# Second mix: gate tiles interleaved with conv tiles; expert tables: one 512-column matmul for high and low x

## The chip, the cores and the metric

The kernel runs on one core of a Trainium2 chip. The metric is device time in microseconds of one execution, here the median of three. TensorE (PE) multiplies, with its weight loads shown apart (PEld); VectorE (DVE), ScalarE (ACT) and GpSimd (POOL) work on what it leaves; SyncE (SP) issues the weight transfers.

## What is computed

Two blocks on 256 tokens of 1024 features. Each has a mixer and then a product-key retrieval over 16384 single-neuron experts. The change touches the second mixer's input projection and the first expert table (`expert_u`) of both blocks:

```python
def second_block(x, ...):
    h = _rmsnorm(x, norm1)
    proj = h @ w_in
    a_q, a_k, a_v, a_beta, a_alpha, a_gate, b_f, b_i, b_q, b_gate, g_a, g_b = _split_cols(proj)
    qkv = _causal_conv_silu(concatenate([a_q, a_k, a_v]), conv_a)    # 4 taps
    o_a = _rmsnorm(_gated_delta_rule(qa, ka, va, beta, log_alpha), a_onorm) * silu(a_gate)
    f_gate = lb + (1.0 - lb) * sigmoid(b_f)
    o_b = _rmsnorm(_hgrn2_recurrence(silu(b_q), 1.0 - f_gate, b_i, log(f_gate)), b_onorm) * sigmoid(b_gate)
    mix = sigmoid(g_a) * (o_a @ w_branch_a) + sigmoid(g_b) * (o_b @ w_branch_b)
    x = x + mix @ w_out
    return x + _peer(_rmsnorm(x, norm2), ...)

def block(xt, it, gt):                       # _peer, for 128 tokens
    h = gelu(einsum('td,tkd->tk', xt, expert_u[it]))
    return einsum('tk,tkd->td', gt * h, expert_v[it])
```

## The kernel before

Both tables are computed densely: scores for all 128 x 128 experts, Gelu, and a gate that is zero where an expert was not chosen. All large products run in three parts, because operands are split into a high and a low piece: high x times high w, low x times high w, high x times low w. A weight tile is 128 x 1024 numbers. `_dma` (L141) fetches it on SP's queue into one of three buffers `raw`; `_conv` (L148) lets ScalarE make `hi` and VectorE or GpSimd make `lo`, cut at column `lo_cut`: VectorE has the columns below it, GpSimd the rest (`CUT` for the tables, `CUT2` for the second mix). `hi` and `lo` have three buffers each, so those of tile e+3 wait for the end of tile e.

`tile_ch` (L178) is one output tile of 128 channels by 256 tokens: for each of 8 chunks of 128 features three matmuls of 256 columns (L187), 24 in a row, into an accumulator `mm` of which there are two. Six more banks (y0 to y3, g0, g1, handed out by `bank`, L123) serve the work that runs beside the tiles.

In `Peer.run` (L552) the first table has 128 tiles, e = 0 to 127. After each, `gelu` (L540) applies the activation on ScalarE, and multiplies on VectorE where the gates are already there; `step` (L196) then lets the background advance by a budget of 1.6 us of estimated VectorE time: first the retrieval (`topk16`, L422, and one-hot rows), then `gates` (L504), which builds the gates by f16 matmuls (L527) of one-hot rows and writes or multiplies them into the scores (L533, L535).

`Mix2.run` (L1389) has 80 input tiles. Before: 24 conv tiles (for each of 8 heads q, k, v), then 8 tiles of the gate a, 8 of f, 8 of q of the second branch, 8 of its gate, 8 of its values, 16 of ga and gb. `conv` (L1006) empties the accumulator into `cvx` on ScalarE, then does three scalar-times-tensor-plus-tensor steps on VectorE (L1013), a sigmoid on ScalarE and a product on VectorE (L1017). `head` (L1019) transposes the result on TensorE (L1025) and takes norms. `both` (L1512) runs the delta rule for heads 0 to 3 and, when all conv tiles are out, for heads 4 to 7. Generators like these advance by a round per `pass_round`, two rounds after each tile.

The order on each engine is not the order of this code alone: a scheduler sets it from the program's dependences. The engines take their instructions strictly in that order.

Of the kernel before, what the change touches and what calls it, by code (L numbers as in the profile page):

```python
# [84 lines left out]
class K:  # L85
    def __init__(self, tc, ins, ctx, plan):
# [4 lines left out]
        self.xh = self.fix.tile([P, NC, T], FR, name="xh")  # L91
        self.xl = self.fix.tile([P, NC, T], FR, name="xl")
# [85 lines left out]
    def tile_ch(self, xh=None, xl=None):  # L178
# [4 lines left out]
        ps = self.ps.tile([P, T], F32, tag="mm", name="mm", bufs=2)  # L183
# [247 lines left out]
class Peer:  # L431
# [108 lines left out]
    def gelu(self, e, ps):  # L540

        nc, n = self.k.nc, self.gated
        a, s = (self.a0, e) if e < SPLIT else (self.a1, e - SPLIT)
        if n < T:
            nc.scalar.activation(out=a[:, s, n:T], in_=ps[:, n:T], func=ACTF.Gelu)  # L545
        if n:
            ge = self.oh.tile([P, T], F32, name="ge", tag="ah", bufs=AB)
            nc.scalar.activation(out=ge[:, 0:n], in_=ps[:, 0:n], func=ACTF.Gelu)
            nc.vector.tensor_tensor(out=a[:, s, 0:n], in0=a[:, s, 0:n], in1=ge[:, 0:n], op=ALU.mult)
        self.acted = e + 1  # L550

    def run(self, after):  # L552
# [3 lines left out]
        with ExitStack() as es:  # L556
# [66 lines left out]
            for e in range(P):  # L623
# [9 lines left out]
                self.gelu(e, k.tile_ch())  # L633
                k.step(BUD[0])
# [257 lines left out]
CUT2 = [384, 640]  # L892
# [9 lines left out]
class Mix2:  # L902
# [14 lines left out]
    def columns(self):  # L917
# [44 lines left out]
        yield  # L962
# [55 lines left out]

    def head(self, h, what, src):  # L1019

        k, nc = self.k, self.k.nc
# [12 lines left out]
        k.done(bt)  # L1034

    def delta(self, g4):
# [5 lines left out]
        ss = self.ssq[g4]  # L1042
        rr = self.t([P, 2, 2, 4], "rr", bufs=2)
# [37 lines left out]
        yield from self.blocks16(lt, X)  # L1081
        lv = self.lev_p.rearrange("p (l n) -> p l n", l=2)
# [306 lines left out]
    def run(self):  # L1389
# [34 lines left out]
        for h in range(H):  # L1424
            for what in range(3):
                ps = k.tile_ch()
                dst = self.t([P, T], "vc", tag="vc", bufs=2) if what == 2 else (self.qc, self.kc)[what][:, h, :]
                self.conv(ps, what * 8 + h, dst)
                k.spawn(self.head(h, what, dst))
                after(2)  # L1430
            if h == 3:
                k.spawn(self.both())
        self.ready.add("qkv")
        k.lo_cut = CUT2[1]
        for h in range(H):
            ps = k.tile_ch()
            silu(ps, self.sga[:, h, :], oa)
            after(2)
        self.ready.add("a_gate")
        for h in range(H):  # L1440
            ps = k.tile_ch()
            self.sigmoid(self.fs[:, h, :], ps)
            after(2)
        for h in range(H):
            ps = k.tile_ch()
            silu(ps, self.qb[:, h, :])
            after(2)
# [64 lines left out]
    def both(self):  # L1512
        yield from self.delta(0)
        while "qkv" not in self.ready:
            yield
# [25 lines left out]

def mix2_out_order():

    for j in range(10):
        if j < 8:
            yield "b", j
        if j > 1:
# [6 lines left out]
MIX2_COLS = ([w * 1024 + h * 128 for h in range(8) for w in range(3)]  # L1554
             + _PART(0) + _PART(1) + _PART(3) + _PART(4) + _PART(2) + _PART(5) + _PART(6))
# [80 lines left out]
```

## Time and profile before

| what | us |
|---|---|
| median of three executions (2248.23 to 2250.43) | 2250.25 |
| the profiled execution | 2248.88 |
| its span, first to last instruction | 2247.1 |
| TensorE busy | 2181.1 (97%) |
| VectorE busy | 1546.5 (69%) |
| ScalarE busy | 1166.4 (52%) |
| GpSimd busy | 829.3 (37%) |

A busy share is an average over stages with different limits. The first table of the first block runs from about 204 to 604 us of the span, that of the second from about 1491 to 1895; the second mix from 955 to 1430 us. Matmuls are pipelined: one has a duration of some 0.28 us, but the next may start 0.12 us later, so the rate is read from the starts, and a stretch that is busy all the time may still be stretched by a lower granted clock (PEclk).

### The profile page before, as it was taken

The page shows a single profiled execution, that of the slowest core. Times are in us where ns is not written, and L with a number is a line of the kernel's source. Part 1 is how long each engine was busy: PE and PEld are TensorE (multiplying, and loading weights), DVE is VectorE, ACT ScalarE, POOL GpSimd, SP SyncE. Part 2 cuts the span into 40 slices and gives each one's busy share as a digit, 9 for nine tenths or more (in the row PEclk, how much of TensorE's full clock was granted, in tenths as well). Part 3 has the DMA queues.
Part 4 walks back from the last instruction along what each step waited for, and adds up shares of the span by engine and source line. Part 5 has one row for each costly group of instructions (what it writes and reads, how often), then busy time and mean ns, then how long its engine had stood idle before and what let it go on. Part 6 is the DMA issues. An engine that isn't in the chain of part 4 may idle for free. (4 is left out here: it accounts for less than half of the span.)

```text
span 2247.1 us, 41435 instructions
## 1 busy us (share of the span) xinstructions
PE 2181.1 (97%) x15512; PEld 2025.8 (90%) x15512; DVE 1546.5 (69%) x3119; ACT 1166.4 (52%) x2210; POOL 829.3 (37%) x626
## 2 busy tenths in 40 slices
PE   8999999999999999988899999999999999999998
PEld 7989999999988888778899898899999999888887
DVE  5659986889544544579756787799778885454444
ACT  5645545444555555565444555455454445555554
POOL 3454000000166666645553675530000001656664
PEclk9999999999999999999999999999999999999999
DMA  5555655555556666633334244555555555666664
GB/s 187 158 172 167 183 174 162 159 160 160 178 191 202 205 191 196 187 101 119 123 104 136 64 132 140 178 165 185 171 168 154 157 160 180 195 204 191 195 195 153
DMA packets 103881, 370.90 MB, mean 165 GB/s; under 512 B 12928, under 2 KB 14080, under 8 KB 103424
## 3 DMA queue, kind: packets, MB, share of 16 engines
q1 hardware_dynamic: 101808, 365.21, 52.1%
q10 hardware_dynamic: 1872, 3.04, 0.4%
q8 instruction: 122, 2.00, 0.4%
q14 instruction: 79, 0.65, 0.1%
HBM read 367.16 MB, written 1.05 MB: 164 GB/s over the span
## 5 line engine op out<-in xcount | busy, mean ns | idle before, releaser
L157 POOL TENSOR_TENSOR lo<-raw,hi 128x384 fp32r<-128x384 f32 (+2 forms) x428 | 702.3, 1643 | 1337.3 <-ACT hi L152 1306.7
L152 ACT ACTIVATE hi<-raw 128x1024 fp32r<-128x1024 f32 x684 | 724.0, 1060 | 693.6 <-PE mm L187 405.9
L187 PE MATMUL mm<-xh,hi 128*128 128x256 f32 x3168 | 918.8, 290 | 15.5 <-ACT cvx L1009 5.7
L187 PE MATMUL mm<-xh,lo 128*128 128x256 f32 x3168 | 902.8, 285 | 0.4 <-DVE lo L157 0.4
L187 PE MATMUL mm<-xl,hi 128*128 128x256 f32 x3168 | 898.8, 284 | 1.3 <-DVE xl L309 1.0
L157 DVE TENSOR_TENSOR lo<-raw,hi 128x640 fp32r<-128x640 f32 (+2 forms) x654 | 665.9, 1019 | 336.1 <-ACT hi L152 331.8
L187 PEld LDWEIGHTS mm<-xh,hi 128*128 128x128 f32 x3168 | 603.4, 190 | 19.6 <-ACT cvx L1009 6.8
L187 PEld LDWEIGHTS mm<-xl,hi 128*128 128x128 f32 x3168 | 604.0, 191 | 2.7 <-DVE xl L309 1.6
L187 PEld LDWEIGHTS mm<-xh,lo 128*128 128x128 f32 x3168 | 599.8, 189 | 0.6 <-DVE lo L157 0.6
L261 PE MATMUL y<-lo,ah 128*128 128x512 f32 x1024 | 398.3, 389 | 0.0
L261 PE MATMUL y<-hi,ah 128*128 128x512 f32 x1024 | 397.4, 389 | 0.0
L261 PE MATMUL y<-hi,al 128*128 128x512 f32 x1024 | 276.0, 389 | 0.0
L617 DVE TENSOR_TENSOR al<-a,ah 128x256 fp32r<-128x256 f32 x256 | 118.7, 464 | 188.8 <-PE y L261 188.5
L261 PEld LDWEIGHTS y<-lo,ah 128*128 128x128 f32 x1024 | 192.2, 188 | 40.2 <-POOL lo L157 0.3
L261 PEld LDWEIGHTS y<-hi,al 128*128 128x128 f32 x1024 | 192.2, 188 | 39.8
L261 PEld LDWEIGHTS y<-hi,ah 128*128 128x128 f32 x1024 | 192.2, 188 | 39.8
L616 ACT ACTIVATE ah<-a 128x256 fp32r<-128x256 f32 x256 | 106.4, 416 | 167.2 <-PE y L261 165.7
L517 DVE TENSOR_TENSOR ow<-ow,w 128x1024 f16<-128x1024 f16 x128 | 87.3, 684 | 0.1
L545 ACT ACTIVATE a<-mm 128x256 f32<-128x256 f32 (+33 forms) x228 | 69.2, 303 | 0.0
L527 PEld LDWEIGHTS <-o 128*128 128x128 f16 x1024 | 59.6, 97 | 6.3
L514 DVE TENSOR_TENSOR ow<-iota,ij 128x1024 f16<-128x1024 f16 x64 | 44.3, 692 | 27.6 <-PE by L527 19.1
L533 DVE TENSOR_TENSOR a<-by,a 128x256 f32<-128x256 f32 (+15 forms) x144 | 47.8, 349 | 11.9 <-PE by L527 11.6
(500 smaller groups left out, 1972.1 us busy)
## 6 DMA issues: line engine op xcount, KB each, us to landing
raw<-in_u_dram SPq DMA_DIRECT2D x256, 512.0 KB, 3.6
raw<-in_v_dram SPq DMA_DIRECT2D x256, 512.0 KB, 4.2
raw<-in_w_in_dram SPq DMA_DIRECT2D x108, 512.0 KB, 3.6
raw<-in_wq_dram SPq DMA_DIRECT2D x32, 512.0 KB, 3.9
raw<-in_w_out_dram SPq DMA_DIRECT2D x16, 512.0 KB, 3.6
raw<-in_w_branch_a_dram SPq DMA_DIRECT2D x8, 512.0 KB, 3.5
raw<-in_w_branch_b_dram SPq DMA_DIRECT2D x8, 512.0 KB, 3.7
skT<-in_sk_dram ACTq DMA_DIRECT2D x2, 1024.0 KB, 5.2
```

Of the source, the lines that this page charges most:

```text
L152: self.nc.scalar.activation(out=h, in_=r, func=ACTF.Copy)
L157: eng.tensor_tensor(out=l[:, a:b], in0=r[:, a:b], in1=h[:, a:b].bitcast(F32), op=ALU.subtract)
L187: self.nc.tensor.matmul(out=ps, lhsT=a[:, c, :], rhs=b, start=(c == 0 and k == 0), stop=(c == NC - 1 and k == 2))
L261: i = self.nc.tensor.matmul(out=self.y[tt][dh], lhsT=p[:, ts], rhs=q[:, ds], start=(first and m == 0), stop=(last and m == 2))
L514: nc.vector.tensor_tensor(out=ow[0], in0=iota, in1=some(self.ij[:, 1]), op=ALU.is_equal)
L517: nc.vector.tensor_tensor(out=ow[q], in0=ow[0], in1=some(self.w[:, q]), op=ALU.mult)
L527: nc.tensor.matmul(out=g[:, n, :], lhsT=hot[n][0], rhs=hot[n][1 + q], start=(q == 0), stop=(q == 1))
L533: nc.vector.tensor_tensor(out=v, in0=gi[:, e:e + hi - lo], in1=v, op=ALU.mult)
L545: nc.scalar.activation(out=a[:, s, n:T], in_=ps[:, n:T], func=ACTF.Gelu)
L616: nc.scalar.activation(out=h, in_=a, func=ACTF.Copy)
L617: nc.vector.tensor_tensor(out=l, in0=a, in1=h.bitcast(F32), op=ALU.subtract)
```

## The change

*Expert tables.* `tile_pair` is a second form of a table tile. High and low x now stand side by side in one buffer `xx`, so one matmul of 512 columns multiplies a chunk of `hi` with both, into the two halves of a bank; one of 256 columns adds high x times `lo` to the first half. ScalarE copies the second half out, VectorE adds the first half to it, and Gelu reads the sum. It is used for every odd tile and for tiles after the background has run out; its step has 0.25 us less budget. The accumulator `mm` is now two whole banks.

*Second mix.* The 24 conv tiles and the 16 tiles of gate a and f come in one mixed order (`mix2_in_order`): a gate tile after every third conv tile for heads 0 to 3, then after every one. `tile_wide` takes one of the six banks as accumulator when at least four are free. `conv` no longer copies into `cvx`: ScalarE's scaled copy and VectorE's three steps read the accumulator itself. The sigmoid, the product and the transposes moved into `head`, behind two further rounds. The delta rule waits for its own heads, and blocks of four heads follow each other without the wait for all conv tiles. While these 40 tiles run, VectorE makes 640 columns of `lo` instead of 384 for the conv tiles. The columns of the weight in memory are permuted to the new order.

```diff
+        self.xx = self.fix.tile([P, NC, 2, T], FR, name="xx")
+        self.xh, self.xl = self.xx[:, :, 0, :], self.xx[:, :, 1, :]
...
+    def tile_pair(self):
+
+        h, l = (a.rearrange("p (c n) -> p c n", c=NC) for a in self.weights())
+        ps = self.ps.tile([P, 2, T], F32, tag="mm", name="mm", bufs=2)
+        for c in range(NC):
+            both = lambda: self.nc.tensor.matmul(out=ps.rearrange("p a t -> p (a t)"), lhsT=h[:, c, :], rhs=self.xx[:, c].rearrange("p a t -> p (a t)"),
+                                                 start=(c == 0), stop=(c == NC - 1))
+            if c < NC - 1:
+                both()
+            self.nc.tensor.matmul(out=ps[:, 0, :], lhsT=l[:, c, :], rhs=self.xh[:, c, :], start=False, stop=False)
+            if c == NC - 1:
+                both()
+        return ps
+
+    def tile_wide(self):
+
+        if len(self.free) < 4:
+            return self.tile_ch(), lambda: None
+        tag = self.free.popleft()
+        return self.tile_ch(tag=tag), lambda: self.done(tag)
...
+        if pair:
+            ps = self.k.tile_pair()
+            nc.scalar.activation(out=ge, in_=ps[:, 1], func=ACTF.Copy)
+            nc.vector.tensor_tensor(out=ge, in0=ps[:, 0], in1=ge, op=ALU.add)
+            ps = ge
+        else:
+            ps = self.k.tile_ch()
...
-                self.gelu(e, k.tile_ch())
-                k.step(BUD[0])
+                pair = e % 2 == 1 or not k.bg
+                self.gelu(e, pair)
+                k.step(BUD[0] - 0.25 * pair)
...
-CUT2 = [384, 640]
+CUT2 = [640, 640]
...
-    def conv(self, ps, n, out):
+    def conv(self, h, what):
+
         k, nc = self.k, self.k.nc
-        c = self.t([P, T], "cvx", tag="hon", bufs=2)
-        nc.scalar.activation(out=c, in_=ps, func=ACTF.Copy)
+        n = what * 8 + h
+        ps, done = k.tile_wide()
         a = self.t([P, T], "cva", tag="c0", bufs=3)
-        nc.scalar.activation(out=a, in_=c, func=ACTF.Copy, scale=self.cw[:, n, 3:4])
+        nc.scalar.activation(out=a, in_=ps, func=ACTF.Copy, scale=self.cw[:, n, 3:4])
         for s in (1, 2, 3):
-            nc.vector.scalar_tensor_tensor(out=a[:, s:T], in0=c[:, 0:T - s], scalar=self.cw[:, n, 3 - s:4 - s], in1=a[:, s:T],
+            nc.vector.scalar_tensor_tensor(out=a[:, s:T], in0=ps[:, 0:T - s], scalar=self.cw[:, n, 3 - s:4 - s], in1=a[:, s:T],
                                            op0=ALU.mult, op1=ALU.add)
+        done()
+        k.spawn(self.head(h, what, a))
+
+    def head(self, h, what, a):
+        k, nc = self.k, self.k.nc
+        yield
+        yield
         s = self.t([P, T], "cvs", tag="c1", bufs=2)
         self.sigmoid(s, a)
-        nc.vector.tensor_tensor(out=out, in0=a, in1=s, op=ALU.mult)
...
+        src = self.t([P, T], "vc", tag="vc", bufs=2) if what == 2 else (self.qc, self.kc)[what][:, h, :]
+        nc.vector.tensor_tensor(out=src, in0=a, in1=s, op=ALU.mult)
+        yield
...
+        while not all(("head", h, what) in self.ready for h in hs for what in range(3)):
+            yield
...
+    conv = [("c", h, what) for h in range(H) for what in range(3)]
+    rest = [("a", h, 0) for h in range(H)] + [("f", h, 0) for h in range(H)]
+    for n, c in enumerate(conv):
+        yield c
+        if n % 3 == 2 or n >= 12:
+            yield rest.pop(0)
```

The order, at three places. First VectorE in the first table, while the retrieval works on its candidates (`cand`, `ct`, `ci`); `lo` is the low piece of a weight tile. Before:

```order
L157 TENSOR_TENSOR lo_2798<-raw_2694,hi_2796 128x1024
L449 TENSOR_TENSOR cand_3013<-st_1728 128x1024 x2
L157 TENSOR_TENSOR lo_2835<-raw_2731,hi_2833 128x1024
L424 MAX ct_2648<-cand_3013 128x8 x8
L157 TENSOR_TENSOR lo_2872<-raw_2763,hi_2870 128x1024
L425 MAX_INDEX ci_2649<-ct_2648,cand_3013 128x8 x6
L157 TENSOR_TENSOR lo_2909<-raw_2800,hi_2907 128x1024
```

Now:

```order
L474 TENSOR_TENSOR cand_3036<-st_1727 128x1024 x2
L179 TENSOR_TENSOR lo_2809<-raw_2710,hi_2807 128x1024
L449 MAX ct_2637<-cand_3036 128x8 x4
L574 TENSOR_TENSOR ge_2781<-mm_2782,ge_2781 128x256
L449 MAX ct_2637<-cand_3036 128x8 x4
L179 TENSOR_TENSOR lo_2841<-raw_2742,hi_2839 128x1024
L450 MAX_INDEX ci_2638<-ct_2637,cand_3036 128x8 x4
L179 TENSOR_TENSOR lo_2873<-raw_2779,hi_2871 128x1024
```

The addition of a paired tile (ge) stands behind the lo of the tile two further on and a batch of search steps, once in two tiles.

Second VectorE in the second mix, where conv tiles run: cva is the running sum of a conv tile, qc, kc and vc its results, wm an accumulator in one of the six banks. Before:

```order
L157 TENSOR_TENSOR lo_11505<-raw_11360,hi_11503 128x384
L1017 TENSOR_TENSOR vc_11387<-cva_11390,cvs_11395 128x256
L1013 SCALAR_TENSOR_TENSOR cva_11440<-cvx_11438,i_conv_a_2_932,cva_11440 128x255
L1013 SCALAR_TENSOR_TENSOR cva_11440<-cvx_11438,i_conv_a_2_932,cva_11440 128x254
L157 TENSOR_TENSOR lo_11552<-raw_11411,hi_11550 128x384
L1013 SCALAR_TENSOR_TENSOR cva_11440<-cvx_11438,i_conv_a_2_932,cva_11440 128x253
L157 TENSOR_TENSOR lo_11600<-raw_11459,hi_11598 128x384
```

Now:

```order
L1049 SCALAR_TENSOR_TENSOR cva_11031<-wm_11006,i_conv_a_2_931,cva_11031 128x254
L1049 SCALAR_TENSOR_TENSOR cva_11031<-wm_11006,i_conv_a_2_931,cva_11031 128x253
L179 TENSOR_TENSOR lo_11139<-raw_11004,hi_11137 128x640
L1466 SCALAR_TENSOR_TENSOR sga_10650<-wm_11060,i_a_onorm_2_935,ss_11085 128x256
L1061 TENSOR_TENSOR vc_11094<-cva_11031,cvs_11092 128x256
L179 TENSOR_TENSOR lo_11182<-raw_11058,hi_11180 128x640
L1049 SCALAR_TENSOR_TENSOR cva_11131<-wm_11106,i_conv_a_2_931,cva_11131 128x255
```

The three steps read wm where they read cvx, and the gate's step (sga) stands among them.

Third TensorE at the end of the second delta group (X, XT, u, vs, kt belong to it; hz to the second branch). Before:

```order
L1121 MATMUL by3_13629<-k_ident_69,X_13108 128x128 x4
L1121 MATMUL by2_13669<-k_ident_69,X_13108 128x128 x4
L1131 MATMUL bg1_13729<-vs_11012,XT_13628 128x128 x4
L1294 MATMUL by3_13761<-hz_13742 128x128
L1134 MATMUL bg0_13734<-XT_13628,kt_11013 128x128 x4
L1294 MATMUL by2_13763<-hz_13752 128x128
L1161 MATMUL by3_13865<-vs_11012,XT_13628 128x128
L1145 MATMUL by0_13798<-u_13728,kt_11013 128x128 x4
```

Now:

```order
L1177 MATMUL by3_13810<-vs_10648,XT_13695 128x128 x4
L1180 MATMUL bg1_13815<-XT_13695,kt_10649 128x128 x4
L1340 MATMUL bg0_13845<-hz_13823 128x128
L1429 MATMUL by2_13849<-k_ident_68,tv_13841 128x128 x2
L212 MATMUL mm_13931<-xx_64,lo_13854 128x256
L212 MATMUL mm_13931<-xx_64,hi_13852 128x256 x2
L1340 MATMUL by1_13847<-hz_13833 128x128
```

Matmuls of an input tile (mm) now stand between the steps of the group, where none stood.

## Rows read from the trace of the kernel before

**Rows 1.** Busy time of each engine in six stretches, with clock and DMA.

```profile
core 0: us, PE busy (x) PEld busy (x) DVE busy (x) ACT busy (x) POOL busy (x), PEclk, DMA share, GB/s
204.00:300.00 96.00, 95.58 (x797) 95.37 (x797) 93.45 (x204) 48.48 (x74) 0.00 (x0) 1.00 0.59 181
440.00:560.00 120.00, 120.00 (x1124) 118.57 (x1123) 108.48 (x201) 55.94 (x140) 0.00 (x0) 1.00 0.53 158
955.00:1110.00 155.00, 130.19 (x980) 125.40 (x981) 133.99 (x251) 89.36 (x216) 81.38 (x60) 0.91 0.37 114
1110.00:1160.00 50.00, 50.00 (x422) 48.27 (x422) 17.21 (x26) 20.43 (x32) 21.34 (x18) 1.00 0.32 96
1160.00:1260.00 100.00, 90.70 (x715) 86.42 (x714) 68.90 (x141) 45.26 (x89) 49.93 (x59) 0.95 0.35 111
1260.00:1390.00 130.00, 124.06 (x1017) 119.11 (x1016) 101.56 (x221) 80.73 (x212) 93.58 (x131) 1.00 0.40 118
```

**Rows 2.** Timeline of TensorE: start us, duration us, line, output and inputs, shapes.

```profile
415.96 0.28 PE L187 MATMUL mm<-xh,lo 128*128 128x256 f32 x1
...
418.48 0.28 PE L187 MATMUL mm<-xh,lo 128*128 128x256 f32 x1
...
751.22 0.39 PE L261 MATMUL y<-lo,ah 128*128 128x512 f32 x1
...
752.58 0.39 PE L261 MATMUL y<-lo,ah 128*128 128x512 f32 x1
```

**Rows 3.** Waits of TensorE, 900 to 1430 us: total us, times, longest.

```profile
PE by L1025 <- DVE kc L1017: 6.3, 5, 4.1
PE bg L1025 <- DVE vc L1017: 5.8, 3, 3.3
PE mm L187 <- ACT cvx L1009: 5.7, 4, 2.5
PE bg L306 <- ACT a L279: 5.5, 1, 5.5
PE mm L187 <- DVE qb L1418: 3.9, 3, 3.3
```

**Rows 4.** Groups on VectorE, 958 to 1160 us: count | busy us, mean ns | idle before.

```profile
L1013 DVE SCALAR_TENSOR_TENSOR cva<-cvx,i_conv_a,cva 128x253 f32<-128x253 f32 x24 | 22.3, 929 | 0.2
L157 DVE TENSOR_TENSOR lo<-raw,hi 128x384 fp32r<-128x384 f32 x23 | 19.7, 858 | 1.7 <-ACT hi L152 1.6
L157 DVE TENSOR_TENSOR lo<-raw,hi 128x640 fp32r<-128x640 f32 x20 | 18.6, 931 | 29.0 <-ACT hi L152 28.5 <-PE mm L187 0.4
L1013 DVE SCALAR_TENSOR_TENSOR cva<-cvx,i_conv_a,cva 128x255 f32<-128x255 f32 x24 | 14.9, 622 | 3.9 <-ACT cva L1011 3.9
L1013 DVE SCALAR_TENSOR_TENSOR cva<-cvx,i_conv_a,cva 128x254 f32<-128x254 f32 x24 | 14.6, 606 | 0.2
```

**Rows 5.** Two lines of code: count, duration ns min/median/max, first and last start.

```profile
L1013 DVE SCALAR_TENSOR_TENSOR cva<-cvx,i_conv_a,cva x72: 388/480/1885, 971.1 to 1082.4; 128x255 f32<-128x255 f32 x24, 128x254 f32<-128x254 f32 x24, 128x253 f32<-128x253 f32 x24
L1420 DVE SCALAR_TENSOR_TENSOR sga<-mm,i_a_onorm,ss x8: 471/477/479, 1084.0 to 1112.5; 128x256 f32<-128x256 f32 x8
```

**Rows 6.** Groups on GpSimd and ScalarE, 958 to 1160 us.

```profile
L157 POOL TENSOR_TENSOR lo<-raw,hi 128x640 fp32r<-128x640 f32 x23 | 40.2, 1751 | 47.7 <-ACT hi L152 30.0 <-DVE kg L980 4.6 <-DVE svm L1237 4.2
L157 POOL TENSOR_TENSOR lo<-raw,hi 128x384 fp32r<-128x384 f32 x20 | 29.2, 1462 | 35.3 <-ACT hi L152 31.2 <-PE by L1025 2.2 <-PE mm L187 1.8
L1009 ACT ACTIVATE cvx<-mm 128x256 f32<-128x256 f32 x24 | 8.9, 371 | 0.0
```

**Rows 7.** Groups on VectorE in the first table, 440 to 560 us.

```profile
L514 DVE TENSOR_TENSOR ow<-iota,ij 128x1024 f16<-128x1024 f16 x16 | 11.1, 693 | 5.0 <-PE by L527 3.8 <-PE bg L527 1.2
L533 DVE TENSOR_TENSOR a<-bg,a 128x256 f32<-128x256 f32 x12 | 5.1, 422 | 2.6 <-PE bg L527 2.5
```

**Rows 8.** Timeline of ScalarE and VectorE during the retrieval; in brackets the wait before.

```profile
235.18 1.06 ACT L152 ACTIVATE hi<-raw 128x1024 fp32r<-128x1024 f32 x1 [1.55 <-PE mm L187]
239.30 1.21 DVE L157 TENSOR_TENSOR lo<-raw,hi 128x1024 fp32r<-128x1024 f32 x1
```

More of the change, by code (lines that the diff above doesn't have):

```diff
@@ L90, in __init__ @@
         self.ps = ctx.enter_context(tc.tile_pool(name="ps", bufs=1, space=PSUM))
-        self.xh = self.fix.tile([P, NC, T], FR, name="xh")
-        self.xl = self.fix.tile([P, NC, T], FR, name="xl")
+        self.xx = self.fix.tile([P, NC, 2, T], FR, name="xx")
+        self.xh, self.xl = self.xx[:, :, 0, :], self.xx[:, :, 1, :]
         self.x = self.fix.tile([P, 2, D], F32, name="x")
@@ L182, in tile_ch @@
         l = l.rearrange("p (c n) -> p c n", c=NC)
-        ps = self.ps.tile([P, T], F32, tag="mm", name="mm", bufs=2)
+        if tag is None:
+            ps = self.ps.tile([P, 2, T], F32, tag="mm", name="mm", bufs=2)[:, 0, :]
+        else:
+            ps = self.ps.tile([P, T], F32, tag=tag, name="wm")
         for c in range(NC):
@@ L538, in gates, with gelu @@
                 yield 0.00105 * TB * self.acted + 0.12
-    def gelu(self, e, ps):
+    def gelu(self, e, pair):
         nc, n = self.k.nc, self.gated
         a, s = (self.a0, e) if e < SPLIT else (self.a1, e - SPLIT)
+        if n or pair:
+            ge = self.oh.tile([P, T], F32, name="ge", tag="ah", bufs=AB)
+        if pair:
[3 more added lines that the diff above has]
+            ps = ge
+        else:
+            ps = self.k.tile_ch()
         if n < T:
@@ L546, in gelu @@
         if n:
-            ge = self.oh.tile([P, T], F32, name="ge", tag="ah", bufs=AB)
             nc.scalar.activation(out=ge[:, 0:n], in_=ps[:, 0:n], func=ACTF.Gelu)
@@ L961, in columns @@
         nc.vector.scalar_tensor_tensor(out=g, in0=g, scalar=-1.0, in1=ex[:, 16:24].unsqueeze(1).to_broadcast([P, 2, H]), op0=ALU.mult, op1=ALU.mult)
-        yield
+        for _ in range(4):
+            yield
         nc.vector.tensor_scalar(out=self.beta, in0=eb, scalar1=1.0, scalar2=None, op0=ALU.add)
@@ L1034, in head @@
         k.done(bt)
+        self.ready.add(("head", h, what))
     def delta(self, g4):
@@ L1081, in delta @@
         yield from self.blocks16(lt, X)
+        yield
+        yield
         lv = self.lev_p.rearrange("p (l n) -> p l n", l=2)
@@ L1423, in run @@
         next(k.spawn(self.columns()))
-        for h in range(H):
-            for what in range(3):
-                ps = k.tile_ch()
[L1427 to L1431, printed above, removed]
+        for kind, h, what in mix2_in_order():
+            if kind == "c":
+                self.conv(h, what)
+            elif kind == "a":
+                ps, done = k.tile_wide()
+                silu(ps, self.sga[:, h, :], oa)
+                done()
+            else:
+                ps = k.tile_ch()
+                self.sigmoid(self.fs[:, h, :], ps)
+            after(2)
+            if (kind, h, what) == ("c", 3, 2):
                 k.spawn(self.both())
-        self.ready.add("qkv")
+        self.ready.add("a_gate")
         k.lo_cut = CUT2[1]
         for h in range(H):
[L1436 to L1445, printed above, removed]
+            ps, done = k.tile_wide()
             silu(ps, self.qb[:, h, :])
+            done()
             after(2)
@@ L1513, in both @@
         yield from self.delta(0)
-        while "qkv" not in self.ready:
-            yield
         yield from self.delta(1)
@@ L1553 @@
 _PART = lambda b: [_A + b * 1024 + h * 128 for h in range(8)]
-MIX2_COLS = ([w * 1024 + h * 128 for h in range(8) for w in range(3)]
-             + _PART(0) + _PART(1) + _PART(3) + _PART(4) + _PART(2) + _PART(5) + _PART(6))
+MIX2_COLS = ([w * 1024 + h * 128 if kind == "c" else _PART("af".index(kind))[h] for kind, h, w in mix2_in_order()]
+             + _PART(3) + _PART(4) + _PART(2) + _PART(5) + _PART(6))
 def program(tc, ins, out):
```

6 lines of the change are left out of this document (3 added, 3 removed).

## The prediction

> **What bounds the kernel now.** I read the page's busy times and slices first: TensorE is busy for 97% of a span of 2247.1 us, so the question is only where it idles and where its instructions stand far apart. The stretches [rows 1] show it. In the expert table (204 to 300 and 440 to 560 us) TensorE is busy all the time at full clock: the stage lasts as long as its matmuls follow each other. In the second mix (955 to 1390 us) it is not: busy 130.19 of 155 us at a mean granted clock of 0.91, then 50 of 50, 90.70 of 100 at 0.95 and 124.06 of 130. The starts of single matmuls [rows 2] give the unit of the sum: 21 steps of 256 columns from 415.96 to 418.48 us are 0.120 us each, 6 steps of 512 columns from 751.22 to 752.58 are 0.227 us each. With 0.120 us for each instruction in [rows 1], the second mix loses: 155 - 980 x 0.120 = 37 us before 1110, nothing from 1110 to 1160 (422 x 0.120 = 51), 100 - 715 x 0.120 = 14 us to 1260, and 130 - 1017 x 0.120 = 8 us to 1390.
>
> The first 37 us are 24.8 idle and 12.6 of slower matmuls at the lower clock. 5.5 of the idle time is the wait for the norm ahead of the stage, which stays. Of the rest the waits of TensorE [rows 3] name the convolution: 6.3 and 5.8 us for the products kc and vc, 5.7 for the copy cvx that empties the accumulator. VectorE is busy for 133.99 of these 155 us, but for 17.21 of the next 50 [rows 1]. So the conv tiles come too densely for VectorE, and the gate tiles behind them leave it idle.
>
> Why VectorE is so slow there is in [rows 4]: the 72 conv steps (L1013) take 22.3 + 14.9 + 14.6 = 51.8 us, 0.72 each. One alone is 0.480 (median), the longest 1.885 [rows 5]. The long ones lie beside GpSimd's instructions, 1.751 us for its 640 columns of lo [rows 6]. The gate's step (L1420) has the same form, but reads the accumulator for one of its two tensors: 0.471 to 0.479 us in all eight [rows 5], though GpSimd works then too.
>
> **The change part by part. Expert tables.** In a paired tile each of the 8 chunks has one matmul of 512 columns for hi and one of 256 for lo, where three of 256 were. A chunk saves 2 x 0.120 - 0.227 = 0.0133 us, a tile 0.106. The order of the changed program has 1040 matmuls of 512 columns in the tables, that is 130 paired tiles, 65 for each expert table: 130 x 0.106 = **13.8 us**, all on the path, since TensorE is full there. [...]
>
> A pair adds a copy on ScalarE (0.37 us, as cvx of the same form in [rows 6]) and an addition on VectorE (0.42 us, as L533 in [rows 7]). ScalarE is half idle in both stretches [rows 1]. VectorE has 93.45 of 96 us while the retrieval runs and 108.48 of 120 while the gates are built. The background's budget is cut by 0.25 us a pair, so its load rises by 0.17 us in two tiles of some 6 us: 3%, covered in the gates and barely in the retrieval. What the addition delays is the accumulator: with two of them, tile e+2 waits until the addition of tile e is done. In the new order it stands behind lo of tile e+2 and a batch of search steps. Now lo runs late: the hi that started at 235.18 us has its lo at 239.30 [rows 8], 4.12 later. That hi starts when tile e-1 ends, 2.88 before the end of tile e; so lo starts 1.24 us after that end, takes 1.2, the batch some 1.3, the addition 0.4: done after 4.1 us, where 2.88 are free. TensorE waits 1.2 us, once, for after it VectorE is no longer as late. With a little for the gates I take 1.5 us for each table, so the tables give **-11 us**; the ends are -13.8 and, if every pair waits as long as it saves, 0.
>
> **Mixed stage, to 1160 us.** The conv steps now read the accumulator: 72 x 0.477 = 34.3 us in place of 51.8, so 17.5 less on VectorE. [...] The cut of lo from 384 to 640 columns gives VectorE 24 x (0.931 - 0.858) = 1.8 us [rows 4] and takes 24 x (1.751 - 1.462) = 6.9 from GpSimd [rows 6]. The 24 copies cvx, 8.9 us, go from ScalarE [rows 6]. VectorE's 134.0 + 17.2 = 151 us up to 1160 become 135, and they are spread over 40 tiles in place of 24 dense and 16 light ones: some 75% of the stretch. The transposes of a head (L1025) stood one to four tiles behind their conv tile in TensorE's order and stand two to five behind it now, and the conv tiles come half as densely. So of the 17.8 us of conv waits I take 70%, 12.5; the lower clock follows such waits (0.91 here, 1.00 where TensorE does not wait), and I take 65% of its 12.6 us, 8. Together **-21 us**. Bounds: 0, if something else than VectorE holds the transposes back; -31, if all but the norm's wait goes. Six banks serve as accumulators when four are free, so a conv tile that holds its bank for three steps (1.4 us) costs TensorE nothing as long as the heads leave some.
>
> **1160 to 1260 us.** The wait for qb, 3.9 us [rows 3], is one for a free accumulator and goes with the wide banks. The last steps of the second delta group stood without a tile between them; now tiles stand there. Of the 14 us I take **-6**, between 0 and -12. From 1260 on the chains of the second branch have their order; I take 0, between -4 and +4.
>
> **The sum.** -11 - 21 - 6 = -38. The profiled execution took 2248.9 us with a span of 2247.1; the median of the runs, 2250.25, is 1.4 above it. 2250.25 - 38 gives **2212 us**, its own range 2200 to 2227.
>
> **Rivals.** *The waits move inside the mix.* The second delta group is emitted only when all its heads are done, and begins some five tiles later than before; wide tiles and heads compete for six banks. If only 8 of the 27 us come, 2231. For it: the part from 1160 on is a chain through ScalarE and VectorE. Against it: VectorE's load falls. *The pairs save nothing:* a matmul of 512 columns beside one of 256 could be paced by its weight load, so that a pair costs 2 x 0.120 us, or the new waits eat the gain: 2250 - 27 = 2223. Against it: [rows 2] have the 512 at 0.227 with a weight load before each. [...] *Slower: VectorE becomes the bound of the tables.* In the gates it is busy for 108.48 of 120 us, and 5.0 + 2.6 us of its gaps are waits for gate matmuls [rows 7], so little is left. If each addition lets it wait for the end of its tile and then sends lo out late, TensorE pays in every pair. From (13.8 + 27)/130 = 0.31 us a pair on, the kernel is slower; at 0.5 us it is 2250 + 130 x 0.5 - 41 = 2274. Against it: those gaps shrink when VectorE is late, and lo has almost two tiles of slack. *Neither part takes:* the scheduler had mixed conv and gate work already, and additions eat the pairs: 2250.
>
> **How the numbers follow.** Forecast 0.66, waits moved 0.14, pairs without gain 0.10, tables bound by VectorE 0.07, neither 0.03. The range runs from 2197 (the forecast's bounds nearly all taken) to 2236 (beyond the waits that move); it leaves out the last two cases and tails. A measurement of this kernel can tell 0.2% from no change, 4.5 us. Faster 0.90, same 0.03, slower 0.07.
>
> **What would show it.** Right: 512-column matmuls in the tables with the next start 0.227 us later; conv steps at 0.48 us with none above 0.6; a first table some 5 us shorter; 955 to 1160 us some 20 shorter, at a clock of 0.95 or more. Wrong: TensorE waiting for VectorE's additions by more than 0.1 us a pair; the heads' transposes waiting 10 us or more in the mix; the time after the mixed stage growing by what the stage saved.

## The result, and the profile after

The changed kernel takes 2227.26 us (median; 2223.96 to 2229.74), the kernel before 2250.34 beside it: a ratio of 0.9898, with a 95% interval of 0.9881 to 0.9915, or 23 us less. The profiled execution has a span of 2225.3 us, 21.8 less than before.

Where the 22 us come from is read from five lines of TensorE: the first search product of each table (skT), the first output product behind each (y), and the first transpose of the norm between the blocks (bg<-a). The columns are count, duration in ns (min/median/max), first and last start in us; the first start is the one to read. In the kernel before:

```profile
L582 PE MATMUL bg<-skT,q x24: 270/275/275, 154.8 to 196.6; 128*128 128x128 f32 x24
L261 PE MATMUL y<-hi,ah x142: 389/389/401, 603.9 to 699.6; 128*128 128x512 f32 x142
L306 PE MATMUL bg<-a x16: 421/421/552, 957.9 to 961.2; 128*128 128x128 f32 x16
L582 PE MATMUL bg<-skT,q x24: 272/275/275, 1442.4 to 1484.4; 128*128 128x128 f32 x24
L261 PE MATMUL y<-hi,ah x101: 389/389/401, 1891.6 to 1959.6; 128*128 128x512 f32 x101
```

The same five in the changed kernel:

```profile
L615 PE MATMUL bg<-skT,q x24: 272/275/275, 156.0 to 197.9; 128*128 128x128 f32 x24
L286 PE MATMUL y<-hi,ah x136: 387/389/397, 608.0 to 699.1; 128*128 128x512 f32 x136
L331 PE MATMUL bg<-a x16: 421/421/552, 961.8 to 965.1; 128*128 128x128 f32 x16
L615 PE MATMUL bg<-skT,q x24: 270/275/275, 1417.5 to 1459.4; 128*128 128x128 f32 x24
L286 PE MATMUL y<-hi,ah x134: 387/389/398, 1869.7 to 1960.0; 128*128 128x512 f32 x134
```

| stretch | before, us | after, us | difference | forecast |
|---|---|---|---|---|
| up to the first search | 154.8 | 156.0 | +1.2 | 0 |
| first search and expert table | 449.1 | 452.0 | +2.9 | -5.5 |
| its output products | 354.0 | 353.8 | -0.2 | 0 |
| second mix, with its norms | 484.5 | 455.7 | -28.8 | -27 |
| second search and expert table | 449.2 | 452.2 | +3.0 | -5.5 |
| output products and end | 355.5 | 355.6 | +0.1 | 0 |

The mixed stage gave what was forecast. The tables, which were to give 11 us, cost 6. The stretches after it answer to [rows 1]; those of the mixed stage are shifted by the 4 us by which it begins later.

```profile
204.00:300.00 96.00, 91.62 (x633) 84.44 (x632) 93.82 (x217) 52.13 (x86) 0.00 (x0) 1.00 0.52 168
440.00:560.00 120.00, 119.11 (x972) 111.07 (x972) 110.25 (x215) 63.17 (x158) 0.00 (x0) 1.00 0.48 160
959.00:1114.00 155.00, 141.34 (x1126) 136.10 (x1127) 111.84 (x235) 83.86 (x185) 68.23 (x57) 0.97 0.38 124
1114.00:1164.00 50.00, 48.87 (x416) 48.67 (x416) 39.24 (x62) 25.40 (x50) 38.12 (x32) 1.00 0.37 120
1164.00:1264.00 100.00, 96.31 (x814) 93.09 (x814) 79.16 (x177) 55.38 (x129) 56.93 (x85) 1.00 0.33 110
1264.00:1394.00 130.00, 124.59 (x965) 117.74 (x965) 102.09 (x194) 75.35 (x179) 87.65 (x104) 1.00 0.42 139
```

TensorE now idles 4.4 of 96 us in the retrieval, where it idled 0.4. In the mixed stage it is busy 141.34 of the first 155 us in place of 130.19, at a granted clock of 0.97 in place of 0.91. That 0.97 is a mean: a lower clock (0.50 from 962.5 to 967.5 us) is granted for parts of the first 40 us only, 0.66 in the ten from 960 us, behind the 5.5 us wait for the norm that ends at 961.8, and from 1000 us to the end of these stretches the clock is 1.00. VectorE's load has moved from there (133.99 to 111.84) into the next 50 us (17.21 to 39.24).

**The tables.** TensorE's waits in the first one, 156 to 608 us (total us, times, longest); before, this stretch had one wait of 0.4 us:

```profile
PE mm L135 <- ACT a L579: 2.6, 2, 1.3
PE mm L135 <- DVE ge L574: 2.4, 5, 1.0
PE mm L135 <- ACT ge L581: 0.9, 1, 0.9
```

These are 5.9 us in eight waits; the second table has 6.4 in seven. All are waits of a paired tile (L135) for its accumulator: until an addition has read it (L574), or until Gelu on ScalarE has (L579 and L581). Two stretches of 20 us show what VectorE, the third of the busy times, does there: it is full, as it was in the kernel before (20.00 and 19.56), and the additions come on top.

```profile
220.00:240.00 20.00, 19.30 (x134) 17.65 (x134) 20.00 (x52) 9.38 (x16) 0.00 (x0) 1.00 0.51 168
240.00:260.00 20.00, 16.37 (x110) 14.67 (x109) 19.48 (x60) 10.26 (x15) 0.00 (x0) 1.00 0.49 159
```

One wait step by step, from the timelines of TensorE, ScalarE and VectorE (start us, duration us):

```profile
237.64 0.39 ACT L573 ACTIVATE ge<-mm 128x256 f32<-128x256 f32 x1 [1.88 <-PE mm L135]
240.34 1.06 ACT L174 ACTIVATE hi<-raw 128x1024 fp32r<-128x1024 f32 x1 [1.36 <-DVE ci L450]
241.31 0.37 ACT L579 ACTIVATE a<-mm 128x256 f32<-128x256 f32 x1
241.82 0.41 DVE L574 TENSOR_TENSOR ge<-mm,ge 128x256 f32<-128x256 f32 x1
```
```profile
240.15 0.28 PE L212 MATMUL mm<-xx,lo 128*128 128x256 f32 x1
241.72 0.50 PE L135 MATMUL mm<-xx,hi 128*128 128x512 f32 x1 [1.30 <-ACT a L579]
```

The copy of a pair begins at 237.64, its addition only at 241.82, behind search steps and low halves. All that time the pair holds one of the two accumulators. So the tile that begins at 241.72 has only the other one, and that is free when ScalarE has applied Gelu to the tile that has just ended (241.31 to 241.68). ScalarE, in its own order, makes the `hi` of a later tile first (240.34, 1.06 us), which makes up most of that delay; putting Gelu ahead of it was not tried. TensorE works on one accumulator: from 240.15 to 241.72 are 1.57 us where 0.12 would be. The wait costs 1.45 us, a little more than the 1.30 shown as idle, and the pair behind it is slower too: it takes 2.92 us from its first matmul to that of the next tile (241.72 to 244.64), a pair without a wait 2.81 (335.12 to 337.93). Six of the eight pairs behind a wait are slower in this way.

The saving is there, but smaller than forecast. Five chunks of a pair, and six chunks of an ordinary tile close by:

```profile
320.42 0.40 PE L212 MATMUL mm<-xx,hi 128*128 128x256 f32 x2
...
322.58 0.40 PE L212 MATMUL mm<-xx,hi 128*128 128x256 f32 x2
...
323.51 0.39 PE L135 MATMUL mm<-xx,hi 128*128 128x512 f32 x1
323.74 0.28 PE L139 MATMUL mm<-xx,lo 128*128 128x256 f32 x1
...
325.26 0.39 PE L135 MATMUL mm<-xx,hi 128*128 128x512 f32 x1
```

A chunk takes (325.26 - 323.51)/5 = 0.350 us in a pair and (322.58 - 320.42)/6 = 0.360 in an ordinary tile. So a pair saves 8 x 0.010 = 0.08 us, 65 of them 5.2 us a table. Eight waits, 5.9 us shown, some 0.15 us more each, and six times 0.11 behind them, cost 7.8. That is +2.6; the table grew by 2.9, and the last 0.3 us I can't place.

**The mixed stage.** The convolution's steps after, beside [rows 5], and the longest waits of TensorE from 904 to 1434 us, beside [rows 3]:

```profile
L1049 DVE SCALAR_TENSOR_TENSOR cva<-wm,i_conv_a,cva x72: 418/476/484, 975.0 to 1140.1; 128x255 f32<-128x255 f32 x24, 128x254 f32<-128x254 f32 x24, 128x253 f32<-128x253 f32 x24
```
```profile
PE bg L331 <- ACT a L304: 5.5, 1, 5.5
PE by L1066 <- DVE qc L1061: 2.0, 1, 2.0
PE wm L212 <- ACT sq L1071: 2.0, 2, 1.1
PE wm L212 <- DVE sga L1466: 1.5, 1, 1.5
```

No step is longer than 0.484 us, where the longest was 1.885. Of the 17.8 us of convolution waits 2.0 are left, and the wait for qb is no longer among the longest.

### The profile page after: what moved, and what is told of

Read it like the earlier page. It is cut to its first block, busy times and chain, and to the rows that moved or that the text cites. A ratio compares the mean times of both kernels' runs of the same rounds, so it can differ in the third digit from the quotient of the medians.

```text
span 2225.3 us, 39602 instructions
## 1 busy us (share of the span) xinstructions
PE 2163.1 (97%) x14472; PEld 1959.3 (88%) x14472; DVE 1567.7 (70%) x3253; ACT 1200.6 (54%) x2321; POOL 820.4 (37%) x626
## 5 line engine op out<-in xcount | busy, mean ns | idle before, releaser
L179 POOL TENSOR_TENSOR lo<-raw,hi 128x384 fp32r<-128x384 f32 (+1 forms) x428 | 691.2, 1617 | 1316.0 <-ACT hi L174 1275.7
L179 DVE TENSOR_TENSOR lo<-raw,hi 128x640 fp32r<-128x640 f32 (+1 forms) x654 | 667.2, 1021 | 280.5 <-ACT hi L174 274.6
L212 PE MATMUL mm<-xx,hi 128*128 128x256 f32 x3616 | 677.6, 286 | 5.7 <-DVE sg L885 3.3
L212 PEld LDWEIGHTS mm<-xx,hi 128*128 128x128 f32 x3616 | 565.2, 189 | 12.1 <-DVE sg L885 3.7
L212 PE MATMUL mm<-xx,lo 128*128 128x256 f32 x1808 | 511.7, 283 | 0.3 <-DVE lo L179 0.2
L135 PE MATMUL mm<-xx,hi 128*128 128x512 f32 x1040 | 384.1, 402 | 12.4 <-ACT a L579 6.8
L212 PEld LDWEIGHTS mm<-xx,lo 128*128 128x128 f32 x1808 | 341.7, 189 | 0.7 <-DVE lo L179 0.7
L139 PE MATMUL mm<-xx,lo 128*128 128x256 f32 x1040 | 270.0, 280 | 0.0
L135 PEld LDWEIGHTS mm<-xx,hi 128*128 128x128 f32 x1040 | 194.6, 187 | 51.1 <-ACT a L579 7.6
L139 PEld LDWEIGHTS mm<-xx,lo 128*128 128x128 f32 x1040 | 195.5, 188 | 5.9
L573 ACT ACTIVATE ge<-mm 128x256 f32<-128x256 f32 x130 | 49.7, 383 | 166.2 <-PE mm L135 156.2
L212 PE MATMUL wm<-xx,hi 128*128 128x256 f32 x640 | 121.7, 288 | 5.2 <-ACT sq L1071 2.0
L212 PEld LDWEIGHTS wm<-xx,hi 128*128 128x128 f32 x640 | 100.1, 191 | 6.5 <-ACT sq L1071 2.4
```

Of the source, the lines that this page charges most:

```text
L135: both = lambda: self.nc.tensor.matmul(out=ps.rearrange("p a t -> p (a t)"), lhsT=h[:, c, :], rhs=self.xx[:, c].rearrange("p a t -> p (a t)"),
L139: self.nc.tensor.matmul(out=ps[:, 0, :], lhsT=l[:, c, :], rhs=self.xh[:, c, :], start=False, stop=False)
L179: eng.tensor_tensor(out=l[:, a:b], in0=r[:, a:b], in1=h[:, a:b].bitcast(F32), op=ALU.subtract)
L212: self.nc.tensor.matmul(out=ps, lhsT=a[:, c, :], rhs=b, start=(c == 0 and k == 0), stop=(c == NC - 1 and k == 2))
L573: nc.scalar.activation(out=ge, in_=ps[:, 1], func=ACTF.Copy)
```

## The experiments on the tables

Each run is told as a ratio to the kernel before, measured beside it.

**No pairs.** One line of the changed kernel:

```diff
-                pair = e % 2 == 1 or not k.bg
+                pair = False
```

> The changed kernel without its pairs: every tile of the two expert tables by three 256-column matmuls a chunk again, the mixed stage as changed. Theory W (the pairs lose in the retrieval what they save): the trace puts the mixed stage at 28.7 us less and both tables at 5.8 us more, so without pairs 2250.3 - 28.7 = 2222, ratio 0.987, both tables back at 444.2 and 460.3 us from the last step before them to their first output matmul. Rival F (the tables do save the 11 us of the forecast, and the 15 us that are missing went somewhere in the mixed stage or behind it): 2227 + 11 = 2238, ratio 0.995.

Measured: 2220.77 us, ratio 0.9868 (0.9854 to 0.9882). In its trace the two tables take 449.2 and 449.3 us again. Theory W holds: the mixed stage alone gives 29 us, and without the pairs the kernel is better by some 6. The two intervals just touch (0.9881 and 0.9882), so this rests on the lengths of the tables as well. The forecast's -11 were not hidden elsewhere.

**Pairs alone.** The kernel before with `tile_pair`, `gelu`, the activation tile `xx` and the loop of the changed one:

```diff
-                self.gelu(e, k.tile_ch())
-                k.step(BUD[0])
+                pair = e % 2 == 1 or not k.bg
+                self.gelu(e, pair)
+                k.step(BUD[0] - 0.25 * pair)
```

> The kernel before with the pairs of the expert tables and the wide activation tile, the mixed stage as before. Theory W: slower, 2250.3 + 6 = 2256, ratio 1.0026, TensorE waiting some 6 us a table for accumulators in the retrieval, in pairs whose addition comes over 2 us after its copy. Rival F: 2250.3 - 11 = 2239, ratio 0.995.

Measured: 2253.97 us, ratio 1.002 (1.0011 to 1.0028): slower by some 4 us. The tables take 451.7 and 451.9 us, with 6.0 and 6.2 us of waits of the same kind. This agrees with the run above from the other side.

**Pairs after the retrieval only.**

```diff
-                pair = e % 2 == 1 or not k.bg
+                pair = closed and (e % 2 == 1 or not k.bg)
```

> The changed kernel with pairs only once the retrieval has ended (about 40 of 65 a table are left), where the additions follow their copies within 1.6 us. Theory W: a pair saves 8 x (0.360 - 0.350) = 0.078 us, 80 pairs 6.3, and only the two waits at the first gates (1 us each) stay: 2222 - 6.3 + 2 = 2218, ratio 0.9855. Rival P (every pair costs, in the gates as in the retrieval, 5.8/130 = 0.045 us each): 2222 + 3.6 = 2225, ratio 0.989.

Measured: 2223.25 us, ratio 0.9882 (0.9868 to 0.9896); tables of 450.6 and 450.6 us. This was a miss: theory W gave 2218, its ratio of 0.9855 lies outside the interval, and rival P's 0.989 lies in it. The retrieval's waits did go, as theory W has it, but others came. In the first table (156 to 606 us):

```profile
PE mm L135 <- ACT ge L581: 3.1, 5, 1.4
PE by L552 <- ACT a L560: 0.7, 1, 0.7
```

While the gates are built, five pairs wait for an accumulator too, here until Gelu has read it; with the pairs placed elsewhere, the scheduler had made another order. So the retrieval is not the cause by itself. Two accumulators are too few for a tile that needs two engines to empty it, here in the gates (3.1 us) as in the retrieval.

**Less background after a pair.**

```diff
-                k.step(BUD[0] - 0.25 * pair)
+                k.step(BUD[0] - (0.25 if closed else 0.7) * pair)
```

> The changed kernel with all its pairs, but after a pair in the retrieval 0.7 us less background work is issued instead of 0.25 us. Theory W, by load: over two tiles VectorE has two low-half subtractions of 1.2 us, 1.6 + 1.35 us of search and 0.4 us of addition, 5.75 us against 5.68 us of TensorE, so it falls behind; with 0.7 us less it is 5.3 us, the additions follow within some 2 us, the waits of 12 us shrink to under 4: 2227 - 9 = 2218, ratio 0.986, and the retrieval ends about a tenth later. Rival P (pairs cost everywhere, not by the retrieval's load): 2227, ratio 0.9898. Rival O (the place of the addition in VectorE's row is what counts, behind the low half of two tiles later, not the load): waits of half their size, 2221 to 2224.

Measured: 2241.66 us, ratio 0.9968 (0.9956 to 0.9979): worse by some 15 us than the change, and none of the three had expected it. Waits in the first table:

```profile
PE y L286 <- ACT ah L649: 3.1, 1, 3.1
PE mm L135 <- ACT a L579: 2.6, 2, 1.3
PE mm L135 <- DVE ge L574: 2.4, 5, 1.0
PE mm L135 <- ACT ge L581: 1.8, 2, 0.9
```

The waits of the retrieval, the second and third line, are the same to a tenth in this table (in the second they are 5.4 us for 5.5). The budget sets how early work is written down, and the scheduler puts it on VectorE as early all the same. What the smaller budget did was to move the last gates to the end of the table, where the output products now wait 3.1 us for them; the tables take 457.6 and 459.2 us. Behind that wait matmuls of the output products last up to 0.794 us, where none is over 0.397 in the changed kernel, and the output products take 3.0 us more. This test of the load failed to change the load, so it tells nothing on theory W, and something on the budget.

**A bank of its own for every pair.** The six banks of the background lend one:

```diff
-        ps = self.ps.tile([P, 2, T], F32, tag="mm", name="mm", bufs=2)
+        tag = self.free.popleft() if len(self.free) > 3 else None
+        if tag is None:
+            ps = self.ps.tile([P, 2, T], F32, tag="mm", name="mm", bufs=2)
+        else:
+            ps = self.ps.tile([P, 2, T], F32, tag=tag, name="wm")
...
             nc.vector.tensor_tensor(out=ge, in0=ps[:, 0], in1=ge, op=ALU.add)
+            if tag is not None:
+                self.k.done(tag)
```

> The changed kernel with every pair of the tables accumulating in one of the six banks that are otherwise the background's (when over three are free), so that its late addition holds up no accumulator. Theory B (what a table loses is the accumulator that a late addition holds): the seven waits of the retrieval and the wait at the gates go, 12 us of both tables, and the saving of 0.078 us a pair stays: 2227 - 12 = 2215, ratio 0.9845. Rival L (VectorE is short of time there, so the low halves, which stand in the same row as the additions, come as late): the waits turn from additions to low halves, 2225 to 2229.

Measured: 2219.49 us, ratio 0.9873 (0.9858 to 0.9887). The tables take 445.3 and 445.4 us, 3.8 less than before the change and 6.7 less than after it. TensorE's waits in the first table:

```profile
PE wm L143 <- DVE lo L183: 0.5, 1, 0.5
PE mm L216 <- ACT hi L178: 0.4, 1, 0.4
```

Theory B holds: no tile waits for an accumulator in it, although VectorE is as busy as in the changed kernel:

```profile
220.00:240.00 20.00, 20.00 (x145) 18.83 (x144) 20.00 (x55) 10.26 (x17) 0.00 (x0) 1.00 0.53 184
240.00:260.00 20.00, 19.45 (x133) 17.45 (x131) 20.00 (x62) 10.39 (x18) 0.00 (x0) 1.00 0.46 160
```

Rival L, by which the low halves would come as late, gets 0.5 us. It is the accumulator that the late addition held, not VectorE's time. The whole gained about 6 us of the 13 that the two tables show; its mixed stage, the same code, was 3.5 us longer in the profiled execution, and the output products 1 us each. By the total it is no better than the kernel without pairs (0.9868).

**And no pair in the last four tiles.**

```diff
-                pair = e % 2 == 1 or not k.bg
+                pair = e % 2 == 1 and e < P - 4
```

> The changed kernel with its pairs in borrowed banks, and no pair in the last four tiles of a table, where the next stage's first activations have to be ready. Theory: the two short waits at the head of the stage after a table (0.27 us each) go, the saving of two or three pairs with them: 2219, the same as with all pairs in borrowed banks, ratio 0.984 to 0.988. If the borrowed banks are as good as the traces of the tables say (13 us less in both tables than the change as it stands), the ratio comes out below 0.987 again.

Measured: 2215.57 us, ratio 0.9854 (0.9839 to 0.987), with tables of 445.3 and 445.5 us, and output products as long as before. It is the fastest of all: 34 us below the kernel before, and its interval does not touch that of the change as it was made. Against the kernel without pairs (0.9868) the intervals overlap, so that the pairs help there is shown by the lengths of the tables, not by the total.

## The experiments on the mixed stage

The first four start from the changed kernel without pairs (0.9868) and undo one part each. The further rounds that the change puts into `head`, `columns` and the delta rule, and the delta rule's wait for its own heads alone, were not undone by themselves: what they give is not shown.

**The copy is back.** The steps read a copy of the accumulator:

```diff
+        c = self.t([P, T], "cvx", tag="hon", bufs=2)
+        nc.scalar.activation(out=c, in_=ps, func=ACTF.Copy)
...
-            nc.vector.scalar_tensor_tensor(out=a[:, s:T], in0=ps[:, 0:T - s], scalar=self.cw[:, n, 3 - s:4 - s], in1=a[:, s:T],
+            nc.vector.scalar_tensor_tensor(out=a[:, s:T], in0=c[:, 0:T - s], scalar=self.cw[:, n, 3 - s:4 - s], in1=a[:, s:T],
```

> The changed mixed stage without pairs (the kernel that measured 2220.8), with one part undone: the convolution's accumulator is copied to the shared buffer first and its three steps read the copy. Theory C (the forecast's largest term): 72 steps go back from 0.477 us to as much as 1.885 us where GpSimd reads the buffers too, some 17 us of VectorE and 24 copies of ScalarE come back: 2221 + 10 (0 to 17), ratio 0.991. Rival N (the new order alone relieves VectorE, 64 tiles' additions lie between): 2221, ratio 0.987.

Measured: 2234.67 us, ratio 0.9941 (0.9929 to 0.9953): 16 us of the 30 are lost. VectorE's groups from 962 to 1165 us (count | busy us, mean ns):

```profile
L1051 DVE SCALAR_TENSOR_TENSOR cva<-cvx,i_conv_a,cva 128x255 f32<-128x255 f32 x24 | 18.2, 762 | 3.5 <-ACT cva L1049 3.5
L1051 DVE SCALAR_TENSOR_TENSOR cva<-cvx,i_conv_a,cva 128x254 f32<-128x254 f32 x24 | 14.8, 619 | 0.4
L1051 DVE SCALAR_TENSOR_TENSOR cva<-cvx,i_conv_a,cva 128x253 f32<-128x253 f32 x24 | 14.3, 599 | 0.3
```

The 72 steps take 47.3 us where they took 34.0 in the run without pairs: 13.3 us of VectorE's time, and some 16 of the kernel's. Theory C holds, at its upper end; the 24 copies on ScalarE come back in the same edit, and the run does not tell the two apart. Steps with both inputs in the buffers go up to 1.297 us in this run and to 1.885 in the kernel before, where 17 of the 72 are longer than 0.5 us and each of these lies beside an instruction of GpSimd. Steps with one input in the accumulator end at 0.484 in the changed kernel, where 36 of the 72 lie beside one.

**The old order of tiles.** `mix2_in_order` gives the 24 convolution tiles first:

```diff
-    for n, c in enumerate(conv):
-        yield c
-        if n % 3 == 2 or n >= 12:
-            yield rest.pop(0)
+    yield from conv + rest
```

> The changed mixed stage without pairs, with the old order of its tiles: the 24 convolution tiles in a row, then a_gate, then f_gate. Theory O (the interleaving spreads VectorE's load: the convolutions fill 955 to 1060 and 1110 to 1160 has VectorE at 17 of 50 us): 8 to 15 us come back, 2229 to 2236, ratio 0.991 to 0.994. Rival C alone (reading the accumulators is what does it): 2221 to 2224.

Measured: 2226.66 us, ratio 0.9906 (0.9892 to 0.992). The order is worth 9 us (0.0038 of 2250), a little under what theory O gave it, and more than the rival did. VectorE is light again behind the convolutions, 29.31 of the 50 us:

```profile
1115.00:1165.00 50.00, 50.00 (x425) 50.00 (x424) 29.31 (x41) 21.93 (x35) 35.99 (x33) 1.00 0.46 148
```

**No borrowed banks.**

```diff
-        if len(self.free) < 4:
+        if True:
             return self.tile_ch(), lambda: None
```

> The changed mixed stage without pairs, with no tile in a borrowed bank: the three steps of a convolution hold one of the two accumulators for some 2 us. Theory A (the borrowed banks are needed, since the steps read the accumulator): TensorE waits for the steps as it waited for the copy (5.7 us and more): 2221 + 6 to 12, ratio 0.990 to 0.992. Rival: the two accumulators do, since a step chain of 1.9 us is shorter than a tile of 2.87 us: 2221 to 2223.

Measured: 2231.55 us, ratio 0.9928 (0.9915 to 0.9941): 13 us. The steps hold an accumulator, and TensorE waits for them (956 to 1434 us):

```profile
PE mm L212 <- DVE cva L1049: 10.5, 8, 4.1
PE mm L212 <- DVE qb L1464: 7.7, 3, 4.8
```

Theory A holds, a little beyond its ratio of 0.992. The wait for qb (3.9 us in the kernel before) is back as well, and twice as long.

**GpSimd's old share.**

```diff
-CUT2 = [640, 640]
+CUT2 = [384, 640]
```

> The changed mixed stage without pairs, with GpSimd's old share of the low halves in it (VectorE 384 of 1024 columns instead of 640). Theory V (VectorE is short in the mixed stage, GpSimd's slower part holds the shared buffers): the larger VectorE share costs VectorE 0.3 us a tile and is only bearable because the convolution reads accumulators; going back changes little, 2219 to 2225. Rival G (GpSimd's 640 columns were what made the low halves late and stretched the steps): 2221 + 5 to 10.

Measured: 2240.62 us, ratio 0.9961 (0.9947 to 0.9974): 21 us, twice what the larger guess allowed, and the largest of the four. This undoes more than the change did: here all 40 tiles have the old share, in the kernel before only the 24 convolution tiles had it. GpSimd has 39 instructions of 640 columns here, 23 in [rows 6]. The longest waits of TensorE besides the norm's, GpSimd's group, and an instruction of VectorE with 8 columns beside the one of GpSimd that runs at the time:

```profile
PE mm L212 <- DVE lo L179: 6.4, 3, 3.3
PE wm L212 <- DVE sga L1466: 5.1, 1, 5.1
```
```profile
L179 POOL TENSOR_TENSOR lo<-raw,hi 128x640 fp32r<-128x640 f32 x39 | 68.1, 1752 | 84.1 <-ACT hi L174 72.0 <-PE wm L212 7.6 <-DVE qc L1061 2.2
```
```profile
1039.39 1.56 POOL L179 TENSOR_TENSOR lo<-raw,hi 128x640 fp32r<-128x640 f32 x1
1039.45 1.52 DVE L1099 TENSOR_SCALAR rr<-rr 128x8 f32<-128x8 f32 x1
```

VectorE's steps of the convolution are as fast as ever (0.484 us at most), but now its low halves come late (6.4 us), and an instruction of 8 columns lasts 1.52 us. The second one of this line lasts 0.985 here, beside 384 columns of GpSimd; with the new share the two last 0.974 and 0.158. GpSimd's 640 columns take 1.752 us each, its 384 columns 1.335 in the run with the new share. Rival G holds as to the late low halves, not as to the steps, and by more than its guess. How the 21 us divide between late low halves, stretched small instructions and the lower clock (0.93 and 0.95 in two stretches, against 0.96 and 0.97) is not settled.

**One part alone, and two.** In the kernel before, first only the copy goes:

```diff
-        c = self.t([P, T], "cvx", tag="hon", bufs=2)
-        nc.scalar.activation(out=c, in_=ps, func=ACTF.Copy)
+        c = ps
```

> The kernel before with one edit: the convolution's steps read the accumulator, no copy; old order, two accumulators, no pairs. Theory I (the parts of the mixed stage need each other): the copy that goes gives some 15 us, and the accumulator that the steps now hold for longer takes 10 or more of them back: 2240 to 2250, ratio 0.996 to 1.0. Rival S (the parts add up by themselves): 2250 - 15 = 2235, ratio 0.993.

Measured: 2237.36 us, ratio 0.9948 (0.9934 to 0.9961): 12 us less, between rival S (2235) and the near end of theory I (2240), so this run alone does not decide between them. Then the share as well:

```diff
-CUT2 = [384, 640]
+CUT2 = [640, 640]
```

> The kernel before with two edits and nothing else: the convolution's steps read the accumulator, and VectorE takes 640 of 1024 columns of the low halves among the convolutions instead of 384, so that GpSimd's instructions there are 384 columns (1.46 us) instead of 640 (1.75 us). Theory H (GpSimd's long instructions hold up VectorE's instructions on the shared buffers, tiny ones too: 128x8 products of 1.12 to 1.25 us in the run with the old share against 0.69): the first edit alone gave 12 us, taking the second out of the finished mixed stage cost 20, so the two together give 12 + 8 to 20: 2218 to 2230. Rival I (the share only pays with the interleaved order and the borrowed banks, since here TensorE waits 16.5 us for accumulators that the steps hold): 2234 to 2240, no better than the first edit alone.

Measured: 2238.07 us, ratio 0.9951 (0.9937 to 0.9965): no gain from the share whose undoing costs 21 us in the finished stage. Rival I holds. The longest wait of the first and of the second, 956 to 1434 us:

```profile
PE mm L187 <- DVE cva L1012: 16.5, 8, 9.3
```
```profile
PE mm L187 <- DVE cva L1012: 13.6, 8, 9.3
```

Both times TensorE waits for the accumulators that the steps hold; that these waits are what hides the gain of the share fits the two lines, and is not shown by a run of its own. Undone one by one, the four parts cost 16 + 9 + 13 + 21 = 59 us, twice the 29 that the mixed stage gives as a whole: their effects overlap, and they can't be added up.

## Why the prediction was right, and where not

- **What bounds the kernel**: right. The gain came from the stretch with idle time (24.8 us) and a low clock (0.91).
- **Tables, the saving**: the term of 13.8 us was too large. It put 0.227 us for the 512 columns, taken from products with another neighbour, and a chunk of 0.347; measured is 0.350 against 0.360, so 130 pairs save 10.4.
- **Tables, the wait**: this is the step that failed. The forecast took one wait of 1.5 us a table, "for after it VectorE is no longer as late". It is late again and again, since it is full to 260 us and beyond 280: eight and seven waits, 5.9 and 6.4 us shown, some 8 each with what they cost around them, in place of 1.5. So -11 became +6. The mechanism, an addition that holds the accumulator, was named in the prediction; what was missing is that two accumulators of which one is held leave TensorE none in reserve: the next pair then waits for Gelu on the other one, and each further late addition can cost a wait of its own. The run with borrowed banks shows that the held accumulator is the cause.
- **The signs**: of those for "right", the shorter first table failed (2.9 us longer, forecast 5 shorter); the starts (0.23 us), the steps and the clock (0.97) came. The one for "wrong", TensorE waiting for additions by more than 0.1 us a pair, missed what happened: the rows that name an addition have (2.4 + 1.3)/130 = 0.03, all waits for an accumulator 12.3/130 = 0.09, and only with what they cost around them is it 0.12.
- **Mixed stage, -27 together**: -28.8. By the forecast's own measure of 0.120 us an instruction, TensorE did 140 instructions more in the first 205 us (17 us, forecast 21), 99 more in the next 100 (12, forecast 6) and 52 fewer in the next 130 (-6, forecast 0); the remaining 6 us come behind these stretches. In the first 155 us the idle time fell from 24.8 to 13.7 us, by 11.1 (forecast 12.5), and the slower matmuls from 12.6 to 6.2 us, by 6.4 (forecast 8), so the mechanism is the one named there. That the sum comes within 2 us is in part luck: the shares of 70% and 65% were guesses, and the stretches behind missed in both directions.
- **The convolution's steps**: right in size (34.0 us in the run without pairs, forecast 34.3) and in effect: undoing this alone cost 16 us, doing it alone gave 12.
- **The share of the low halves** was priced as a load of 1.8 us on VectorE and 6.9 off GpSimd. That giving it up costs 21 us in the finished stage was not seen; which of the waits it removes there is not shown.
- **The banks** were said to cost TensorE nothing "as long as the heads leave some". They did, and without them 13 us go.
- **The rivals**: of "the pairs save nothing", the half by which new waits eat the gain came true, and went further; that the weight load paces the 512 columns did not (a chunk of 0.350 us, where one of three matmuls takes 0.360). VectorE as the bound of every pair did not come: in the first table from 320 us on, every addition begins within 1.6 us of the end of its copy, and one pair alone has to wait for an accumulator (at 535.78). The total, 2227.3, lies just above the forecast's own range (2200 to 2227) and 15 us above its 2212; the tables, 17 us off, account for all of that.

## What to carry to other kernels

Work that is moved from the full engine to another one is paid for by what it holds until it is done, not by its length: look up whether that engine is full just there, and give the result a buffer that nobody waits for before saving a tenth of a microsecond a tile. Where VectorE and GpSimd work at the same time, look at how long VectorE's instructions last beside GpSimd's, down to the smallest ones (1.52 us for 8 columns here, beside 1.56 of GpSimd); moving one operand to the accumulator took the steps out of that (0.484 us at most, where 1.885 was). And parts of a change that clear the same stretch don't add up: test them by undoing one in the finished kernel too, since one done alone can show nothing (0 us) whose undoing costs 21 in company.

## What the hardware showed that was not expected

- A matmul of 512 columns with one of 256 beside it starts the next 0.23 us later, and the two take 0.350, where 0.227 and 0.120, together 0.347, had been read from uniform rows.
- An instruction of 128 x 8 numbers on VectorE took 1.52 us beside 640 columns of GpSimd's low half (1.56 us) and 0.985 beside 384 columns; in the changed kernel it took 0.971 beside 384 columns (1.004 us) and 0.157 where no low half ran.
- Reading the accumulator costs VectorE nothing here: steps of 255 columns that no GpSimd instruction overlaps take 0.47 to 0.48 us from it, in the changed kernel, and 0.47 to 0.49, all but one of 0.39, from the buffers in the kernel before. The 0.480 in [rows 5], the median of free and delayed steps together, was close to that.
